# Sums of a second and third matmul operand formed from transposed tiles instead of transposed after they are formed

## The chip, the core and the metric

The kernel runs on one core of a Trainium2 chip. The metric is the device time of one execution in microseconds (us). Engines are named as the profile names them: PE is TensorE (PEld its weight load), DVE is VectorE, ACT is ScalarE, POOL is GpSimd and SP is SyncE.

## What is computed

One layer of a bidirectional encoder on 1024 tokens of width 1024, in float32:

```python
def rmsnorm(x, g):
    y = xf * lax.rsqrt(jnp.mean(xf * xf, axis=-1, keepdims=True) + NORM_EPS)
    return y * g
def swiglu(x, w_gate, w_up, w_down):
    return (jax.nn.silu(x @ w_gate) * (x @ w_up)) @ w_down
...
    h = swiglu(rmsnorm(x, ffn1_pre_g), ffn1_w_gate, ffn1_w_up, ffn1_w_down)   # 1024 -> 2816 -> 1024
    x = x + 0.5 * rmsnorm(h, ffn1_post_g)
    h = rmsnorm(x, mix_pre_g)
    qkv = (h @ w_qkv) ...                     # 16 heads of 64: 8 neighbourhood, 8 dilated
    ...
    mixed = jnp.concatenate([o_na, o_dil], axis=-1) @ w_out
    x = x + rmsnorm(mixed, mix_post_g)
    h = swiglu(rmsnorm(x, ffn2_pre_g), ffn2_w_gate, ffn2_w_up, ffn2_w_down)
    x = x + 0.5 * rmsnorm(h, ffn2_post_g)
```

Three normalised activations are multiplied with wide weights: ahead of the first feed-forward net, ahead of the q/k/v projection, and ahead of the second net. Below they are the first, the second and the third operand.

## The kernel before

**Products.** A float32 operand is kept as a high part, rounded to the type that TensorE multiplies (fp32r), and a low part, the remainder. `mm3` (L274) makes one product from three matmuls: high by high, high by low, low by high. The large products are cut into 2 by 2 blocks and done in seven passes of a Strassen scheme in Winograd's form. The seven left blocks made of an operand are A11, A12, A22 and S1 = A21 + A22, S2 = S1 - A11, S3 = A11 - A21, S4 = A12 - S2.

**Class `Operand`** makes these blocks, one row tile of 128 tokens at a time. Tiles 0 to 3 are upper ones and give A11 and A12; tiles 4 to 7 are lower ones, with the halves a1 (of A21) and a2 (of A22). For each pair of tiles, `squares` (L207) takes sums of squares on ACT (L172), writing their elements into the buffer `xn` that the normalised tile will use; there are two `xn` buffers. `scale` (L217) makes the reciprocal root on DVE by some twelve operations of about 0.2 us (L147 to L158, "the chain" below), and `tile` (L221) writes the normalised tile to `xn` (L225). An upper tile is saved to DRAM at once (L228, POOL's queue). For a lower tile, `sums` (L234) loads the upper one of the same columns back (`x1`, L242) and forms S1 to S4 in `s` on DVE (L248). With `c.deep` at 1, as it is for the second and third operand, there is one `x1` and one `s`, and the next lower tile's load is issued when the tile before has been turned to its last block.

**Turning.** `transpose_in` (L175) turns 128x512 values of a tile: four transposes on PE into one PSUM bank `trp` (L180, "a block" below), the high part from it on ACT (L181), and the low part on DVE (L182). An upper tile takes two blocks, a lower one five. `put` (L252) queues one step for each, and PE's order is written by hand: the matmul loops call `c.step()` after every second `mm3` group, which takes one pending sum and one step from their queues. The order on ACT, DVE and POOL is that in which the framework's scheduler places the instructions. Every engine runs its own list in order.

**Where the operands are made.** The second operand's upper tiles are turned inside the last passes of the first net, its lower ones inside the value and the first q/k passes. The third's upper ones are turned in the out-projection, its lower ones in `ahead` (L411), which runs the first passes of the second net by A11 and A12 while the other blocks are not there yet. In `ahead`, a product by A11 fills a PSUM bank, `save` (L443, `keep` L387) copies it out on ACT (L389) and stores it through POOL's queue, and the product by A12 is added to the same bank. Weight blocks come in through SP's queue (`graw`, L397) and are split to `whi` on ACT (L370) and `wlo` on DVE (L371). `Finish.rest` (L770) loads a tile of the residual (L778), adds the post-norm to it (L781) and stores it (L783), both through POOL's queue.

Of the kernel before, what the change touches and what calls it, by code (L numbers as in the profile page):

```python
# [10 lines left out]
F32 = mybir.dt.float32  # L11
# [8 lines left out]
P, T = 128, 512  # L20
# [9 lines left out]
A11, S2, S1, S4, A12, S3, A22 = range(7)  # L30
# [5 lines left out]
class Ctx:  # L36


    def __init__(self, tc):
        self.tc, self.nc = tc, tc.nc  # L40
        self.todo = deque()
        self.units, self.fillers = deque(), deque()
        self.left, self.rate, self.debt = 0, 0, 0
        self.steps, self.sums, self.pace = deque(), deque(), 1
# [130 lines left out]
def transpose_in(c, x, hi, lo, tag="tr", pool=None):  # L175

    nc = c.nc
    ps = (pool or c.pst).tile([P, 4, P], F32, tag=tag, name="trp")
    for j in range(4):
        nc.tensor.transpose(ps[:, j, :], x[:, j * P:(j + 1) * P], c.ident)  # L180
    nc.scalar.copy(hi, ps)  # L181
    nc.vector.tensor_sub(lo, ps, hi.bitcast(F32))  # L182


class Operand:

    def __init__(self, c, gain, which):
        self.c, self.gain, self.x, self.parts, self.wait, self.open, self.pinned = c, gain, {}, {}, deque(), 0, False  # L190
        for b in (A11, A12):
            self.x[b] = [c.xa.tile([P, 4, T], F32R, tag=f"x{b}{i}", name=f"x{b}{i}") for i in range(2)]
        self.saved = [c.dr.tile([P, D], F32, name=f"xn{which}_{t}") for t in range(4)]
# [27 lines left out]
    def tile(self, t, x, xn, r):  # L221
        c, nc = self.c, self.c.nc
        if xn is None:
            xn = c.xp.tile([P, D], F32, tag="xn", name="xn", bufs=c.xn)
        nc.vector.scalar_tensor_tensor(xn, x, r, self.gain, op0=ALU.mult, op1=ALU.mult)  # L225
        a1, a2 = xn[:, :T], xn[:, T:]
        if t < 4:
            nc.gpsimd.dma_start(self.saved[t], xn)  # L228
            self.parts[t] = deque(((A11, a1), (A12, a2)))
        else:  # L230
            self.wait.append((t, a1, a2))
            self.sums()

    def sums(self):  # L234

        c, nc = self.c, self.c.nc
        if not self.wait or self.open == c.deep:
            return
        self.open += 1
        t, a1, a2 = self.wait.popleft()  # L240
        x1 = c.xp.tile([P, D], F32, tag="x1", name="x1", bufs=c.deep)
        nc.gpsimd.dma_start(x1, self.saved[t - 4])  # L242
        s = c.xp.tile([P, 4, T], F32, tag="s", name="s", bufs=c.deep)
        a11, a12 = x1[:, :T], x1[:, T:]
        s1, s2, s3, s4 = [s[:, i, :] for i in range(4)]
        add, sub = nc.vector.tensor_add, nc.vector.tensor_sub
        for f, *args in ((add, s1, a1, a2), (sub, s2, s1, a11), (sub, s3, a11, a1), (sub, s4, a12, s2)):
            c.sums.append(lambda f=f, args=args: self.pin(lambda: f(*args)))  # L248
        parts = deque(((A22, a2), (S1, s1), (S2, s2), (S3, s3), (S4, s4)))
        c.sums.append(lambda: self.parts.__setitem__(t, parts))  # L250

    def put(self, t):  # L252

        for i in range(5 if t >= 4 else 2):
            self.c.steps.append(lambda: self.one(t))

    def one(self, t):
        while not self.parts.get(t):
            self.c.sums.popleft()()
        b, src = self.parts[t].popleft()  # L260
        cols = slice(t % 4 * P, t % 4 * P + P)
        transpose_in(self.c, src, *[h[:, :, cols] for h in self.x[b]])
        if t >= 4 and not self.parts[t]:
            self.open -= 1
            self.sums()


def load_gain(c, g, tag):
# [79 lines left out]
class PairGemm:  # L348
# [17 lines left out]
    def split(self, raw, tag, pool=None, place=None):  # L366
        c, nc = self.c, self.c.nc
        hi, lo = place() if place else [(pool or c.wr).tile(list(raw.shape), F32R, tag=tag + p, name="w" + p)
                                        for p in ("hi", "lo")]
        nc.scalar.copy(hi, raw)  # L370
        nc.vector.tensor_sub(lo, raw, hi.bitcast(F32))  # L371
        return hi, lo
# [113 lines left out]
    def run(self, final=None, ahead=None):  # L486
# [3 lines left out]
        for b in range(self.n):  # L490
            w, early = self.w.pop(b), b < self.early
            direct, second, sums, rest = self.prepare(b + 1)
            if early:
                s1 = sp.tile([P, T], F32, tag="s1", name="s1")
# [233 lines left out]
class Finish:  # L728
# [22 lines left out]
    def end(self, t, h):  # L751

        c, nc = self.c, self.c.nc
        x, (q, k) = self.xt[t - 4], [self.q[:, i, t - 4:t - 3] for i in range(2)]
        y, v, e = [c.small.tile([P, 4], F32, tag=n, name=n)[:, :1] for n in ("y", "v", "e")]
        nc.vector.tensor_scalar(q, self.ss[:, t, 1:2], 1.0 / D, EPS, op0=ALU.mult, op1=ALU.add)
        nc.scalar.activation(y, self.ss[:, t, 0:1], AF.Sqrt, bias=q, scale=1.0 / D)
        nc.vector.tensor_scalar(k, q, -0.5, None, op0=ALU.mult)
        nc.vector.scalar_tensor_tensor(v, self.ss[:, t, 0:1], -0.5 / D, k, op0=ALU.mult, op1=ALU.add)
        nc.vector.reciprocal(y, y)  # L760
        nc.vector.scalar_tensor_tensor(e, y, v, y, op0=ALU.mult, op1=ALU.mult)
        nc.vector.scalar_tensor_tensor(y, e, 1.5, y, op0=ALU.add, op1=ALU.mult)
# [193 lines left out]
class Unit:  # L956
# [15 lines left out]
    def turn(self):  # L972
        c = self.c
        self.tps = c.pst.tile([P, 4, P], F32, tag="tr", name="ptp")
        for j in range(self.n):
            c.nc.tensor.transpose(self.tps[:, j, :], self.probs[:, j * P:(j + 1) * P], c.ident)  # L976
# [300 lines left out]
def layer(tc, a, out):  # L1277
    nc = tc.nc
    c = Ctx(tc)
    with ExitStack() as ctx:  # L1280
# [3 lines left out]
        def sub():  # L1284
            return ctx.enter_context(ExitStack())
# [18 lines left out]
        x1 = [c.dr.tile([P, D], F32, name=f"x1_{t}") for t in range(8)]  # L1304
# [6 lines left out]
        def right(w, ts, where):  # L1311

            def get(i):
                q = {k: ts[i][j] for j, k in enumerate((T1, T3, T2, T4))}
                for (g, u), k in zip(((0, 0), (0, 1), (1, 1)), (B11, B21, B22)):
                    ch = where(i)[u]
                    q[k] = w[g, ch // 2][:, ch % 2 * T:ch % 2 * T + T]
                return q
            return get
# [144 lines left out]
        s1, s2, xas = sub(), sub(), sub()  # L1464
# [3 lines left out]
        with ExitStack() as order:  # L1468
# [6 lines left out]
                    xs[t] = c.xp.tile([P, D], F32, tag="x", name="x", bufs=4)  # L1475
                    q.dma_start(xs[t], x0[t])
            xs = {}
            op0 = Operand(c, None, 0)

            def begin(pg):  # L1480
                row, eps, ss = c.xp.tile([P, D + P], F32, tag="s", name="row", bufs=2), *[
# [284 lines left out]
        s7, s3, s4, s5 = sub(), sub(), sub(), sub()  # L1766
# [203 lines left out]
```

## Time and profile before

| | before |
|---|---|
| median of 3 runs (lowest to highest) | 1868.24 us (1865.01 to 1870.01) |
| the profiled execution, and its span | 1868.1 us, 1866.1 us |
| PE busy | 1838.7 us (99%) |
| PEld busy | 1534.3 us (82%) |
| DVE busy | 1318.9 us (71%) |
| ACT busy | 795.5 us (43%) |
| POOL busy | 324.8 us (17%) |

Busy is the time in which at least one instruction of the engine ran; the span runs from the first to the last instruction. Matmuls overlap each other: one takes about 0.39 us and the next starts 0.23 us after it. The share of PE is one over the whole program, so what a change is worth has to be read at the place where it stands.

### The profile page before, as it was taken

The numbers are of one execution on the slowest core, as the hardware profiler recorded it, in microseconds if no ns is written. First come the engines' busy times: TensorE is split into PE (matmuls) and PEld (weight loads), VectorE is DVE, ScalarE is ACT, GpSimd is POOL, SyncE is SP. The second block draws the span as 40 slices with busy tenths as digits, with TensorE's granted clock in tenths as the row PEclk, the third lists the DMA queues.
The fourth block names the chain that finished last, engine by engine and source line by source line (L and its number), as shares of the span: only waits on it lengthen the run. The fifth ranks groups of instructions, "written<-read, shape, count | busy, mean of one in ns | idle before, by whom it ended". The sixth has DMA issues, their size and how long they took to land.

```text
span 1866.1 us, 25121 instructions
## 1 busy us (share of the span) xinstructions
PE 1838.7 (99%) x9048; PEld 1534.3 (82%) x9048; DVE 1318.9 (71%) x2208; ACT 795.5 (43%) x1300; POOL 324.8 (17%) x521
## 2 busy tenths in 40 slices
PE   8999999999999999999999999999999999999998
PEld 6888878888888887888899988778888888888886
DVE  6778776777565877577766766785878777754557
ACT  5522233334443645233477765453222333344333
POOL 2101221223000122222442300121111111110000
PEclk9999999999999999999999999999999999999999
DMA  7655467788986756656883732585455656586564
GB/s 267 226 172 192 154 210 240 227 250 274 343 288 210 269 189 225 230 160 222 295 288 111 249 137 81 193 297 175 158 191 184 239 207 233 193 319 206 195 225 148
DMA packets 164990, 404.63 MB, mean 217 GB/s; under 512 B 18881, under 2 KB 35489, under 8 KB 162818
## 3 DMA queue, kind: packets, MB, share of 16 engines
q1 hardware_dynamic: 115664, 228.30, 36.9%
q0 software_dynamic: 48336, 172.63, 26.5%
q10 hardware_dynamic: 866, 2.10, 0.3%
q8 instruction: 71, 1.16, 0.3%
q14 instruction: 53, 0.43, 0.1%
HBM read 276.95 MB, written 131.07 MB: 219 GB/s over the span
## 4 chain that ended last, share of the span: by engine, by line
PE 81%; issue 10%; DVE 4%; DMA 2%; ACT 2%; POOL 0%; DVEq 0%; ACTq 0%; SPq 0%; POOLq 0%
PE mmp L276 17%; PE mmp L278 17%; PE mmp L277 17%; PE accp L276 7%; PE accp L278 7%; PE accp L277 7%; PE po L1088 3%; PE ptp L976 2%; PE po L1209 1%; PE trp L180 1%; PE sp L1076 1%; PE sp L1196 1%; DMA xn<-xn 0%; DMA sgd<-sg 0%; DVE x L182 0%
## 5 line engine op out<-in xcount | busy, mean ns | idle before, releaser
L276 PE MATMUL mmp<-x,whi 128*128 128x512 f32 x1412 | 559.0, 396 | 3.3 <-DVE v L507 1.8
L278 PE MATMUL mmp<-x,wlo 128*128 128x512 f32 x1412 | 553.7, 392 | 0.0
L277 PE MATMUL mmp<-x,whi 128*128 128x512 f32 x1412 | 552.3, 391 | 0.2 <-DVE x L1551 0.2
L276 PEld LDWEIGHTS mmp<-x,whi 128*128 128x128 f32 x1412 | 265.1, 188 | 62.8 <-issue 5.7
L278 PEld LDWEIGHTS mmp<-x,wlo 128*128 128x128 f32 x1412 | 264.9, 188 | 61.0 <-DVE wlo L371 0.7
L277 PEld LDWEIGHTS mmp<-x,whi 128*128 128x128 f32 x1412 | 265.2, 188 | 57.3 <-DVE x L1551 0.5
L648 DVE TENSOR_TENSOR pw<-praw,pw 128x1024 fp32r<-128x1024 f32 (+1 forms) x182 | 199.0, 1138 | 124.5 <-ACT pw L647 124.1
L370 ACT CAST whi<-wraw 128x1024 fp32r<-128x1024 f32 x126 | 132.2, 1052 | 336.1 <-PE mmp L277 276.0
L647 ACT CAST pw<-praw 128x1024 fp32r<-128x1024 f32 (+1 forms) x182 | 169.0, 982 | 204.0 <-PE accp L278 157.6
L276 PE MATMUL accp<-pw 128*128 128x512 f32 x600 | 234.4, 391 | 0.7 <-DVE hb L719 0.7
L278 PE MATMUL accp<-pw 128*128 128x512 f32 x600 | 233.5, 389 | 0.0
L277 PE MATMUL accp<-pw 128*128 128x512 f32 x600 | 233.4, 389 | 0.0
L371 DVE TENSOR_TENSOR wlo<-wraw,whi 128x1024 fp32r<-128x1024 f32 x126 | 154.4, 1227 | 20.2 <-ACT whi L370 20.1
L276 PEld LDWEIGHTS accp<-pw 128*128 128x128 f32 x600 | 112.6, 188 | 24.4 <-issue 1.1
L278 PEld LDWEIGHTS accp<-pw 128*128 128x128 f32 x600 | 112.6, 188 | 23.5
L277 PEld LDWEIGHTS accp<-pw 128*128 128x128 f32 x600 | 112.7, 188 | 23.2
L580 POOL DMA_DIRECT2D g<-sg x44 | 24.1, 547 | 410.7 <-DVE sg L573 232.6
L389 ACT COPY s<-mmp 128x512 f32<-128x512 f32 x52 | 30.6, 588 | 131.0 <-PE mmp L278 121.1
L182 DVE TENSOR_TENSOR x<-trp,x 128x512 fp32r<-128x512 f32 x76 | 52.1, 687 | 26.2 <-ACT x L181 26.1
L181 ACT CAST x<-trp 128x512 fp32r<-128x512 f32 x76 | 44.5, 587 | 46.1 <-PE trp L180 46.1
L461 DVE TENSOR_TENSOR wraw<-wraw 128x1024 f32<-128x1024 f32 x52 | 63.4, 1220 | 0.7
L536 DVE TENSOR_TENSOR c<-mmp,u 128x512 f32<-128x512 f32 x52 | 35.7, 686 | 38.6 <-PE mmp L278 38.5
(288 smaller groups left out, 2789.6 us busy)
## 6 DMA issues: line engine op xcount, KB each, us to landing
praw<-g SPq DMA_DIRECT2D x70, 512.0 KB
wraw<-in_wg_dram SPq DMA_DIRECT2D x44, 512.0 KB
wraw<-in_wu_dram SPq DMA_DIRECT2D x44, 512.0 KB
tr<-in_wd_dram SPq DMA_DIRECT2D x44, 512.0 KB
g<-sg POOLq DMA_DIRECT2D x88, 256.0 KB, 4.5
ts<-tr POOLq DMA_DIRECT2D x22, 1024.0 KB, 4.9
praw<-ts SPq DMA_DIRECT2D x88, 256.0 KB
praw<-in_wd_dram SPq DMA_DIRECT2D x66, 256.0 KB
```

Of the source, the lines that this page charges most:

```text
L181: nc.scalar.copy(hi, ps)
L182: nc.vector.tensor_sub(lo, ps, hi.bitcast(F32))
L276: nc.tensor.matmul(out, ahi, bhi, start=start, stop=False, skip_group_check=go_on)
L277: nc.tensor.matmul(out, ahi, blo, start=False, stop=False, skip_group_check=go_on)
L278: nc.tensor.matmul(out, alo, bhi, start=False, stop=stop, skip_group_check=go_on)
L370: nc.scalar.copy(hi, raw)
L371: nc.vector.tensor_sub(lo, raw, hi.bitcast(F32))
L461: nc.vector.tensor_sub(r[:, 0:2], r[:, 1:3], r[:, 0:2])
L647: nc.scalar.copy(w[side][:, 0, :m], raw[:, :m])
L648: nc.vector.tensor_sub(w[side][:, 1, :m], raw[:, :m], w[side][:, 0, :m].bitcast(F32))
L976: c.nc.tensor.transpose(self.tps[:, j, :], self.probs[:, j * P:(j + 1) * P], c.ident)
L1088: nc.tensor.matmul(po[0][:, un * 2 + j], u.pt[:, 2 * j + t, :], rhs, start=t == 0, stop=t == 1)
```

## The change

It applies to the second and the third operand (`turned=True`); the first is built with `turned=False` and goes on as before.

- An upper tile's block is copied back on ACT from PSUM into `xn` in its transposed form, and the save to DRAM is issued after both blocks, so that what is saved is the transposed tile.
- A lower tile is turned in two blocks in place of five: `left` turns a1 and takes S3 from PSUM, `right` turns a2, splits A22, and forms S2, S1 and S4 on DVE from the turned values. The four sums are split afterwards from `s` in SBUF: high part on ACT, low part on DVE.
- The next lower tile's `x1` is loaded after S4 of the tile before; its sums cannot be formed before its turn on PE. `put` queues two steps and two empty ones for a lower tile.

```diff
         if t < 4:
-            nc.gpsimd.dma_start(self.saved[t], xn)
-            self.parts[t] = deque(((A11, a1), (A12, a2)))
+            if not self.turned:
+                nc.gpsimd.dma_start(self.saved[t], xn)
+            self.parts[t] = deque(lambda b=b, src=src: self.plain(t, b, src) for b, src in ((A11, a1), (A12, a2)))
+            if self.turned:
+                self.parts[t].append(lambda: nc.gpsimd.dma_start(self.saved[t], xn))
...
+    def split(self, t, b, src):
+        nc = self.c.nc
+        hi, lo = self.cols(t, b)
+        nc.scalar.copy(hi, src)
+        nc.vector.tensor_sub(lo, src, hi.bitcast(F32))
+
+    def plain(self, t, b, src):
+        ps = self.turn(src)
+        self.split(t, b, ps)
+        if self.turned:
+            self.c.nc.scalar.copy(src.rearrange("p (k c) -> p k c", k=4), ps)
...
+        def left():
+            while self.splits:
+                c.sums.popleft()()
+            new = place()
+            s.extend(new[:, i].rearrange("p (k c) -> p k c", k=4) for i in range(4))
+            sub(s[2], a11, self.turn(a1))
+
+        def later(b, x):
+            self.splits -= 1
+            self.pin(lambda: self.split(t, b, x))
+
+        def right():
+            s1, s2, s3, s4 = s
+            ps = self.turn(a2)
+            self.split(t, A22, ps)
+            sub(s2, ps, s3)
+            add(s1, s2, a11)
+            sub(s4, a12, s2)
+            self.end()
+            self.splits = 4
+            c.sums.extend(lambda b=b, x=x: later(b, x) for b, x in ((S2, s2), (S3, s3), (S1, s1), (S4, s4)))
+        self.parts[t] = deque((left, right))
...
-        for i in range(5 if t >= 4 else 2):
+        for i in range(5 if t >= 4 and not self.turned else 2):
             self.c.steps.append(lambda: self.one(t))
+        if t >= 4 and self.turned:
+            self.c.steps.extend([lambda: None] * 2)
```

Line numbers differ between the two programs: in the changed one the transposes are L244, the split L250 and L251, the copy back L257, the late save L233, the reload L267, the sums L290 to L302, the weight splits L431 and L432, the copy of `keep` L450, the residual's lines L839 to L844, and the q/k rotation L981 (before: L920). Three places show how the order on the engines moves.

First, POOL's queue in the out-projection, where the third operand's upper tiles 0 and 1 (`xn2_0`, `xn2_1`) are saved and the residual's tiles 2 and 3 (`x2_2`, `x2_3`) are stored. Before:

```order
L228 DMA xn2_0_10768<-xn_11033 128x1024
L228 DMA xn2_1_10769<-xn_11034 128x1024
L783 DMA x2_2_103<-x_11061 128x1024
L783 DMA x2_3_104<-x_11062 128x1024
L242 DMA x1_11460<-xn2_0_10768 128x1024
```

The changed kernel:

```order
L233 DMA xn2_0_10716<-xn_10981 128x1024
L844 DMA x2_2_103<-x_11009 128x1024
L844 DMA x2_3_104<-x_11010 128x1024
L233 DMA xn2_1_10717<-xn_10982 128x1024
L267 DMA x1_11416<-xn2_0_10716 128x1024
```

The save of tile 1 has moved behind the stores of residual tiles 2 and 3.

Second, ACT's list at the start of `ahead`. `trp_11284` (now `trp_11238`) is the last block of the upper tile 3; the `whi` are high parts of the first weight blocks; `s1` is the copy of the first product by A11 out of its PSUM bank; the activation into `xn` is the square of tile 4. Before:

```order
L181 CAST x40_10766<-trp_11284 128x4x128
L370 CAST whi_11324<-graw_11189 128x1024
L370 CAST whi_11367<-graw_11263 128x1024
L389 COPY s1_11344<-mmp_11330 128x512
L370 CAST whi_11410<-graw_11328 128x1024
L172 ACTIVATE xn_11424,ss_11423<-x_11363 128x1024
L389 COPY s1_11387<-mmp_11373 128x512
```

The changed kernel:

```order
L431 CAST whi_11280<-graw_11141 128x1024
L431 CAST whi_11323<-graw_11216 128x1024
L257 COPY xn_11115<-trp_11238 128x512
L431 CAST whi_11366<-graw_11284 128x1024
L172 ACTIVATE xn_11380,ss_11379<-x_11319 128x1024
L450 COPY s1_11300<-mmp_11286 128x512
```

The first copy of `s1` stood behind two weight splits; it stands now behind three, the copy back of tile 3 and the square of tile 4.

Third, DVE's list where the second operand's tiles 6 and 7 get their chain, ahead of the turning of tile 6. `x31` is the low part of block S4 of tile 5, `qk` a product of an earlier pass, `wlo` low parts of weights. Before:

```order
L371 TENSOR_TENSOR wlo_5834<-graw_5739,whi_5833 128x1024
L147 TENSOR_SCALAR v_5864<-ss_5846 128x2
L148 TENSOR_SCALAR y_5865<-v_5864 128x2
L149 TENSOR_SCALAR y_5865<-y_5865 128x2
L182 TENSOR_TENSOR x31_5431<-trp_5851,x30_5430 128x4x128
L156 TENSOR_TENSOR e_5866<-y_5865,v_5864 128x2
```

The changed kernel:

```order
L251 TENSOR_TENSOR x21_5433<-s_5762,x20_5432 128x4x128
L147 TENSOR_SCALAR v_5876<-ss_5823 128x2
L432 TENSOR_TENSOR wlo_5862<-graw_5753,whi_5861 128x1024
L981 TENSOR_TENSOR qk_5856<-qk_5856 128x512
L251 TENSOR_TENSOR x31_5439<-s_5762,x30_5438 128x4x128
L148 TENSOR_SCALAR y_5877<-v_5876 128x2
```

After the chain's first operation (L147) there stand now a weight split, a q/k product and a low part, and the other eleven operations come behind them; before, the chain went on at once with one low part in between.

## Rows read from the trace of the kernel before

**Rows 1.** The page: engines and TensorE clock.

```profile
PE 1838.7 (99%) x9048; PEld 1534.3 (82%) x9048; DVE 1318.9 (71%) x2208; ACT 795.5 (43%) x1300; POOL 324.8 (17%) x521
...
PEclk9999999999999999999999999999999999999999
```

**Rows 2.** Waits of PE: engine, line, releaser: us in total, times, longest.

```profile
PE trp L180 <- DVE xn L225: 2.3, 2, 1.7
...
PE trp L180 <- DVE s L248: 1.5, 1, 1.5
...
PE trp L180 <- DVE x L182: 1.1, 4, 0.4
```

**Rows 3.** Timeline of PE at third operand's tile 2: start, us, instruction.

```profile
1206.91 0.39 PE L278 MATMUL accp<-whi,n 128*128 128x512 f32 x1
...
1207.14 0.60 PE L180 MATMUL trp<-ident,xn 128*128 128x128 f32 x4
...
1207.82 0.39 PE L277 MATMUL accp<-wlo,n 128*128 128x512 f32 x1
```

**Rows 4.** Timeline of PE at second operand's tile 6; idle before in brackets.

```profile
720.02 0.63 PE L180 MATMUL trp<-ident,xn 128*128 128x128 f32 x4 [0.56 <-DVE xn L225]
...
723.55 0.63 PE L180 MATMUL trp<-ident,s 128*128 128x128 f32 x4 [1.52 <-DVE s L248]
```

**Rows 5.** Timeline of ACT and DVE ahead of that tile.

```profile
717.85 1.05 ACT L370 CAST whi<-graw 128x1024 fp32r<-128x1024 f32 x1 [1.26 <-PE mmp L277]
...
719.44 0.62 ACT L919 CAST qk<-qk 128x512 fp32r<-128x512 f32 x1
...
720.99 0.68 DVE L920 TENSOR_TENSOR qk<-qk 128x512 fp32r<-128x512 f32 x1
...
721.59 1.22 DVE L371 TENSOR_TENSOR wlo<-graw,whi 128x1024 fp32r<-128x1024 f32 x1
...
723.33 0.68 DVE L182 TENSOR_TENSOR x<-trp,x 128x512 fp32r<-128x512 f32 x1
```

**Rows 6.** Timeline of ACT, DVE and POOL around the third operand's upper saves.

```profile
1200.08 1.06 ACT L172 ACTIVATE xn<-x 128x1024 f32<-128x1024 f32 x1 [1.70 <-DMA xn<-xn]
...
1201.32 1.06 ACT L172 ACTIVATE xn<-x 128x1024 f32<-128x1024 f32 x1
...
1198.86 1.29 DVE L781 SCALAR_TENSOR_TENSOR x<-hs,y,x 128x1024 f32<-128x1024 f32 x1 [1.00 <-DMA x<-x]
...
1202.50 0.17 DVE L147 TENSOR_SCALAR v<-ss 128x2 f32<-128x2 f32 x1 [1.76 <-ACT xn L172]
...
1204.88 1.29 DVE L225 SCALAR_TENSOR_TENSOR xn<-x,y,gain 128x1024 f32<-128x1024 f32 x1
...
1193.78 1.07 POOL L228 DMA_DIRECT2D xn<-xn  x2
```

**Rows 7.** Line L228, the saves: issue to landing.

```profile
DMA to landing us min/median/max: 4.4/5.2/6.9
```

**Rows 8.** Timeline of ACT and PE at the start of the third operand's passes.

```profile
1216.00 0.59 ACT L389 COPY s<-mmp 128x512 f32<-128x512 f32 x1
...
1219.99 1.05 ACT L370 CAST whi<-graw 128x1024 fp32r<-128x1024 f32 x1 [3.41 <-DMA graw<-in_wg_dram]
...
1220.95 1.06 ACT L172 ACTIVATE xn<-x 128x1024 f32<-128x1024 f32 x1
...
1218.73 0.39 PE L276 MATMUL mmp<-x,w 128*128 128x512 f32 x1
```

**Rows 9.** Timeline of PE, DVE and ACT at second operand's tile 2.

```profile
657.66 0.60 PE L180 MATMUL trp<-ident,xn 128*128 128x128 f32 x4
...
655.45 2.48 DVE L225 SCALAR_TENSOR_TENSOR xn<-x,y,gain 128x1024 f32<-128x1024 f32 x2
...
639.72 1.05 ACT L647 CAST pw<-praw 128x1024 fp32r<-128x1024 f32 x1
```

**Rows 10.** Line L242, the reloads: issue to landing.

```profile
DMA to landing us min/median/max: 4.3/6.0/10.5
```

More of the change, by code (lines that the diff above doesn't have):

```diff
@@ L185, with __init__ @@
 class Operand:
-    def __init__(self, c, gain, which):
+    def __init__(self, c, gain, which, turned=True):
         self.c, self.gain, self.x, self.parts, self.wait, self.open, self.pinned = c, gain, {}, {}, deque(), 0, False
+        self.turned, self.splits = turned, 0
         for b in (A11, A12):
@@ L232, in tile, with cols, turn @@
             self.sums()
+    def cols(self, t, b):
+        return [h[:, :, t % 4 * P:t % 4 * P + P] for h in self.x[b]]
+    def turn(self, src):
+        ps = self.c.pst.tile([P, 4, P], F32, tag="tr", name="trp")
+        for j in range(4):
+            self.c.nc.tensor.transpose(ps[:, j, :], src[:, j * P:(j + 1) * P], self.c.ident)
+        return ps
+    def split(self, t, b, src):
[8 more added lines that the diff above has]
+            self.c.nc.scalar.copy(src.rearrange("p (k c) -> p k c", k=4), ps)
     def sums(self):
@@ L242, in sums @@
         nc.gpsimd.dma_start(x1, self.saved[t - 4])
-        s = c.xp.tile([P, 4, T], F32, tag="s", name="s", bufs=c.deep)
-        a11, a12 = x1[:, :T], x1[:, T:]
-        s1, s2, s3, s4 = [s[:, i, :] for i in range(4)]
         add, sub = nc.vector.tensor_add, nc.vector.tensor_sub
-        for f, *args in ((add, s1, a1, a2), (sub, s2, s1, a11), (sub, s3, a11, a1), (sub, s4, a12, s2)):
-            c.sums.append(lambda f=f, args=args: self.pin(lambda: f(*args)))
-        parts = deque(((A22, a2), (S1, s1), (S2, s2), (S3, s3), (S4, s4)))
@@ L250, in sums, with place @@
-        c.sums.append(lambda: self.parts.__setitem__(t, parts))
+        def place():
+            return c.xp.tile([P, 4, T], F32, tag="s", name="s", bufs=c.deep)
+        if not self.turned:
+            s = place()
+            a11, a12 = x1[:, :T], x1[:, T:]
+            s1, s2, s3, s4 = [s[:, i, :] for i in range(4)]
+            for f, *args in ((add, s1, a1, a2), (sub, s2, s1, a11), (sub, s3, a11, a1), (sub, s4, a12, s2)):
+                c.sums.append(lambda f=f, args=args: self.pin(lambda: f(*args)))
+            parts = deque(lambda b=b, src=src: self.plain(t, b, src)
+                          for b, src in ((A22, a2), (S1, s1), (S2, s2), (S3, s3), (S4, s4)))
+            c.sums.append(lambda: self.parts.__setitem__(t, parts))
+            return
@@ new lines, in sums @@
+        a11, a12 = [x1[:, i * T:i * T + T].rearrange("p (k c) -> p k c", k=4) for i in range(2)]
+        s = []
+        def left():
[17 more added lines that the diff above has]
+            c.sums.extend(lambda b=b, x=x: later(b, x) for b, x in ((S2, s2), (S3, s3), (S1, s1), (S4, s4)))
@@ L252, in put, with end @@
+        self.parts[t] = deque((left, right))
+    def end(self):
+        self.open -= 1
+        self.sums()
     def put(self, t):
-        for i in range(5 if t >= 4 else 2):
+        for i in range(5 if t >= 4 and not self.turned else 2):
             self.c.steps.append(lambda: self.one(t))
+        if t >= 4 and self.turned:
+            self.c.steps.extend([lambda: None] * 2)
     def one(self, t):
@@ L259, in one @@
             self.c.sums.popleft()()
[L260 to L265, printed above, removed]
+        self.parts[t].popleft()()
+        if t < 4 and self.turned and len(self.parts[t]) == 1:
+            self.parts[t].popleft()()
+        if t >= 4 and not self.turned and not self.parts[t]:
+            self.end()
 def load_gain(c, g, tag):
@@ L1477, in layer @@
             xs = {}
-            op0 = Operand(c, None, 0)
+            op0 = Operand(c, None, 0, False)
             def begin(pg):
```

## Prediction

> **What bounds the kernel now.** I read the page first. PE is busy for 99% of the span, at a granted clock that stays at the upper of its two levels (2.4 GHz) in every slice [rows 1]. A PE instruction that falls away is therefore worth its time, and a wait of PE costs its length, unless something else was already holding PE there. DVE (71%) and ACT (43%) have room on average, but the average says nothing of the few us around a row tile. So I went next to the waits of PE: for the blocks of transposes (L180) only small ones are left, 2.3 us for a normalised tile, 1.5 for a sum and 1.1 for a low part that still had to be read out of the PSUM bank [rows 2]. Last I read the timeline at the places where the order of the changed program differs, engine by engine, and followed there what would come late.
>
> **What the change removes.** Eight lower tiles lose three blocks each: 24 blocks. One block in the stream of matmuls costs the distance between the matmul ahead of it and the second one behind it, 1207.82 - 1206.91 = 0.91 us, less two matmul steps of 0.227: 0.455 us [rows 3]. 24 of them are 10.9 us. Waits fall away with them: the 1.52 for a sum and the 0.56 for a normalised tile at the second operand's tile 6 [rows 4], and of the four waits of 1.1 us for low parts about 0.7 (three of the four stand in the third operand) [rows 2]. The 1.7 for the third operand's first tile stays. Together 10.9 + 2.8 = 13.7 us, which is the gain if nothing comes late.
>
> **What it adds at no cost.** Sixteen copies on ACT: no row of before shows one; the nearest is the high part taken from the same bank, and the s1 copy of the same size takes 0.59 us [rows 8]. That is 9.4 us on an engine that is busy for 43%, and it costs nothing by itself; what it costs is order. The lower tiles' DVE work keeps its number of operations.
>
> **What it makes late.** Five places; at each I take what waits, and from when.
>
> First, the second operand's tile 6. PE wanted it at 720.02 - 0.56 = 719.46 [rows 4]. In the changed order the chain for tiles 6 and 7 stands behind a weight low part, whose high part on ACT starts at 717.85, because PE releases its buffer only then, and ends at 718.90, and behind a q/k product, whose ACT part ends at 720.06 [rows 5]. From 718.9 on: low part 1.22 to 720.1, q/k 0.68, low part of S4 0.68 [rows 5] to 721.5, eleven operations of the chain at 2.38 / 12 = 0.2 (twelve run from 1202.50 to 1204.88) [rows 6] to 723.7, normalised tile 1.28 (as L225 takes, 2.48 for two less what overlaps) [rows 9] to 725.0. Stall 5.5 us; at least 3, if the S4 part or the product goes elsewhere, at most 7.
>
> Second, the third operand's tile 2, which PE wanted at 1207.14 [rows 3]. The square of tile 3 writes the `xn` buffer of tile 1 and so waits for that tile's save. Before, the saves were issued at 1193.78, and the square of tile 2 started at 1200.08, on the landing [rows 6]. Now tile 1's save follows both blocks, both copies, and in POOL's queue the store of residual tile 3, whose DVE part ends at 1198.86 + 1.29 = 1200.15. The low part of tile 1's second block comes behind that on DVE (0.69), the copy behind the low part (0.59): save at 1201.4. Landing takes 5.2 (4.4 to 6.9) [rows 7]: 1206.6. Then square 1.06 and its read-out to 1207.9, chain 2.4 with one residual product between (0.7), to 1211.1, tile 1.28: 1212.4. Stall 5.2; 4.4 with the shortest landing, 7 with the longest, 3 if the copy does not wait for the low part and the store.
> The Trainium skill, "DMA: Bandwidth & Descriptors", section "Anatomy of one DMA", puts a transfer from POOL's queue at about 2.0 us and its bytes over 436 GB/s; for 512 KB that is an estimate of 3.2 us. The trace disagrees: 4.4 is the least of eight. By the page this term would be 3.2 in place of 5.2.
>
> Third, the start of `ahead`. The product by A12 is added to the bank that the first s1 copy must read, and PE starts it at 1218.73; the copy was done at 1216.59 [rows 8]. Now that copy stands behind the third weight split and the square of tile 4. The split waits for its load until 1219.99, then 1.05 and 1.06 us for split and square bring 1222.0, with the read-out 1222.2, and the copy 0.59 more [rows 8]. PE goes on at about 1223.1: stall 4.4. If the load came 2 us earlier, 2.4; 6 if the square waits for the save of tile 2.
>
> Fourth, the second operand's tile 2, wanted at 657.66; its normalised tile was ready at 655.45 + 1.28 = 656.7 [rows 9]. Tile 0's second copy stands behind a weight split that ended at 640.77 [rows 9], so save 0 goes out at about 641.4 and lands at 646.6 [rows 7]; only then run the square of tile 2 and, behind it on ACT, tile 1's second copy (1.2 and 0.6), and save 1 follows at 648.5. It lands 5.2 later, and square, chain and tile (4.9) with a weight split between (0.7) end at about 659.4. Stall 1.7, take 2.0; 0 to 3.4.
>
> Fifth, the reloads of `x1`. Blocks of one tile are 1.83 us apart (two groups of `mm3`, 1.37, and a block). The next reload is issued after S4 of the tile before: second block 1.83, high part 0.59, low part and three sums at 0.69, some 5.2 us after that tile's first block. The next tile's first block follows 2 x 1.83 + 2 x 1.37 = 6.4 us after it, so a landing of 6.0 (4.3 to 10.5) [rows 10] holds DVE at S3 for about 4.8 us. PE feels of that only what a weight low part behind it comes late, some 6 us of landing later: 0 at the median, 4.5 at the longest. For three such places and for two low parts queued behind the sums I take 4 together; 0 to 9.
>
> **The sum.** 1868.1 - 13.7 + 5.5 + 5.2 + 4.4 + 2.0 + 4.0 = 1875.5 us. The profiled execution is 0.1 us from the median of the runs, so nothing is added for that. 0.3%, about what a measurement of this kernel can tell from no change, is 5.6 us: the stalls decide at 8.1 (below it faster) and 19.3 (above it slower); I have 21.1.
>
> **The rivals.**
> The transfers land quickly. With the shortest rows, 4.4 and 4.3, the second term is 4.4, the fourth 1.2, the fifth some 1.5 (the two low parts): 1868.1 - 13.7 + 5.5 + 4.4 + 4.4 + 1.2 + 1.5 = 1871.4, no measurable change. For it: the place of the fifth is a median that just hides. Against it: DMA is busy around these places, and eight saves never took less. Chance 0.30, with any other way in which a third of the stalls is hidden (1863 to 1873). The page of the Trainium skill named above would make the landings shorter still, and lead into this rival.
> One stall absorbs the next. PE waiting gives ACT, DVE and the queues time, so that of each operand only the longest wait is paid: 5.5 and 5.2, in all 10.7, 1865.1. If the weight buffer ahead of tile 6 is free 2.6 us earlier (its split idled 1.26 for PE [rows 5]), tile 6 costs 2.9, and it is 1862.5, faster; at no stall 1854.4. Against it: each of the waits hangs on something that PE itself releases or that follows PE's own blocks, so a late PE makes it late too. Chance of ending below 1862.6: 0.17.
> Landings at their longest, 6.9 and 10.5, bring 7, 3.4 and 9 in the second, fourth and fifth terms: 1884 us. Chance 0.08.
>
> **How the numbers follow.** The forecast, five stalls at about their size and slower by 3 to 14 us, has 0.45, its own range 1871 to 1882; with the longest landings, slower holds 0.53. No change 0.30, faster 0.17. The range leaves out the lower part of the faster case and the upper end of the slower one: 1861 to 1885.
>
> **What would show it.** Right: 96 transposes fewer among PE's 9048 instructions [rows 1]; waits of PE for the normalised tile of 5 us or so at two places, and one of some 4 us for the s1 copy. Steps wrong: if the waits of L244 are under 2 us, the saves or the chain are not late; if PE's wait for the s1 copy is missing, ACT was not held. The prediction fails if these three are together under 8 us, or if a stall stands somewhere that none of the five names.

## The result and the profile after

The changed kernel takes 1878.9 us in the median of four runs (1875.96 to 1881.64); before takes 1869.12 in four runs (1865.01 to 1870.09). The ratio is 1.0058, with a 95% interval of 1.0045 to 1.007: slower by 9.8 us in the medians. The forecast was 1875.5 and slower, range 1861 to 1885.

The page of the changed kernel, busy time of each engine and the granted TensorE clock by slices, answers to [rows 1]:

```profile
PE 1835.4 (98%) x8952; PEld 1528.1 (81%) x8952; DVE 1318.4 (70%) x2208; ACT 803.0 (43%) x1316; POOL 323.9 (17%) x521
...
PEclk9999999999999999999999999999999999999999
```

PE runs 96 fewer transposes and is busy 3 us less, and the program is nevertheless longer: the difference is idle time of PE. The tenths of the clock still read 9 in every slice; slices of 47 us are too coarse for what is shown below. The waits of PE in the changed kernel (engine, line, releaser; us in total, times, longest) answer to [rows 2]; L244 are the transposes, L450 is the s1 copy, L337 and L338 are matmuls:

```profile
PE trp L244 <- DVE xn L226: 11.6, 4, 5.5
...
PE mmp L337 <- ACT s L450: 5.6, 2, 4.4
...
PE accp L338 <- DVE pw L709: 1.3, 2, 0.8
...
PE accp L337 <- ACT pw L708: 0.9, 1, 0.9
PE mmp L339 <- DVE pw L432: 0.8, 1, 0.8
...
PE trp L244 <- DVE x L251: 0.4, 1, 0.4
```

Waits for a normalised tile went from 2.3 us to 11.6, and one for an s1 copy appeared with 4.4; those for sums of a lower tile are gone, and those for low parts of the operand shrank to one, in the first operand. The wait of 0.8 us for a weight's low part (L432) is new; it comes some 6 us after the second operand's tile 4 has been turned. Two lines on the value weights (`pw`) are new too: they stand at the hand-off from the q/k passes to the value passes, which no term of the sum had:

```profile
755.55 0.50 PE L338 MATMUL accp<-pw,x 128*128 128x512 f32 x1 [0.52 <-DVE pw L709]
...
757.86 0.50 PE L337 MATMUL accp<-pw,x 128*128 128x512 f32 x1 [0.88 <-ACT pw L708]
...
759.12 0.50 PE L338 MATMUL accp<-pw,x 128*128 128x512 f32 x1 [0.76 <-DVE pw L709]
```

To see where the time went, each matmul of the changed program was laid beside the same one of the kernel before (transposes left out), and the distance between their starts read at the ends of each operand's stretch. The distance grows from 3.2 to 7.9 us over the second operand (the matmuls that before start between 630 and 762) and from 7.0 to 12.8 over the third (1185 to 1300). So the second cost 4.7 us and the third 5.7, in this one run. The first 3.2 us arise in the first net, where the change adds nothing; other runs of the same code show from -0.2 to 5.5 us there, so it is taken for scatter and not for the change. An idle time of PE shows in these distances with some 0.16 us more than its length, since the matmuls on its two sides, which else overlap (0.39 us long, 0.23 apart), no longer do: the 0.52 and 0.88 us above appear as 0.68 and 1.04.

### The profile page after: what moved, and what is told of

It reads as the page before. It is cut to its first block, busy times and chain, and to the rows that moved or that the text cites. A ratio compares the mean times of both kernels' runs of the same rounds, so it can differ in the third digit from the quotient of the medians.

```text
span 1877.8 us, 24958 instructions
## 1 busy us (share of the span) xinstructions
PE 1835.4 (98%) x8952; PEld 1528.1 (81%) x8952; DVE 1318.4 (70%) x2208; ACT 803.0 (43%) x1316; POOL 323.9 (17%) x521
## 4 chain that ended last, share of the span: by engine, by line
PE 82%; DMA 9%; DVE 5%; ACT 2%; issue 2%; SPq 0%; DVEq 0%; POOL 0%; ACTq 0%; POOLq 0%
PE mmp L337 14%; PE mmp L339 14%; PE mmp L338 14%; PE accp L338 10%; PE accp L339 10%; PE accp L337 10%; DMA tr<-in_wd_dram 4%; PE po L1149 3%; DMA ts<-tr 2%; PE ptp L1037 2%; PE po L1270 1%; PE sp L1137 1%; PE trp L244 1%; DMA xn<-xn 1%; PE sp L1257 1%
## 5 line engine op out<-in xcount | busy, mean ns | idle before, releaser
L337 PE MATMUL mmp<-x,whi 128*128 128x512 f32 x1412 | 558.6, 396 | 4.7 <-ACT u L450 1.4
L338 PE MATMUL mmp<-x,whi 128*128 128x512 f32 x1412 | 553.0, 392 | 0.2 <-DVE x L1612 0.2
L337 PEld LDWEIGHTS mmp<-x,whi 128*128 128x128 f32 x1412 | 265.3, 188 | 67.3 <-issue 5.4
L338 PEld LDWEIGHTS mmp<-x,whi 128*128 128x128 f32 x1412 | 265.4, 188 | 58.1 <-DVE x L1612 0.5
L431 ACT CAST whi<-wraw 128x1024 fp32r<-128x1024 f32 x126 | 132.2, 1051 | 325.3 <-PE mmp L338 254.2
L337 PE MATMUL accp<-pw 128*128 128x512 f32 x600 | 234.2, 390 | 0.0
L338 PE MATMUL accp<-pw 128*128 128x512 f32 x600 | 233.4, 389 | 0.0
L432 DVE TENSOR_TENSOR wlo<-wraw,whi 128x1024 fp32r<-128x1024 f32 x126 | 153.6, 1221 | 17.6 <-ACT whi L431 17.5
L337 PEld LDWEIGHTS accp<-pw 128*128 128x128 f32 x600 | 112.6, 188 | 23.3
L338 PEld LDWEIGHTS accp<-pw 128*128 128x128 f32 x600 | 112.6, 188 | 23.1
L450 ACT COPY s<-mmp 128x512 f32<-128x512 f32 x52 | 30.5, 587 | 125.6 <-PE mmp L339 115.9
L402 DVE TENSOR_TENSOR tr<-tr 128x1024 f32<-128x1024 f32 x26 | 31.8, 1221 | 48.1 <-DMA tr<-in_wd_dram 40.8
L431 ACT CAST whi<-traw 128x512 fp32r<-128x512 f32 x52 | 32.2, 620 | 55.0 <-DVE traw L523 55.0
```

The source lines that it names most:

```text
L337: nc.tensor.matmul(out, ahi, bhi, start=start, stop=False, skip_group_check=go_on)
L338: nc.tensor.matmul(out, ahi, blo, start=False, stop=False, skip_group_check=go_on)
L402: nc.vector.tensor_sub(r[:, 0:2], r[:, 1:3], r[:, 0:2])
```

## The experiments

All ratios are to the kernel before in the same set of runs; the changed kernel has four runs, the others four to twelve. The last two columns are the growth of that distance over the two stretches, from the one profiled run of each kernel, where a few tenths are not meaningful. The hand-off alone takes 2.7 to 3.0 us of the second column wherever the second operand is changed, and more in two runs: 4.6 with the s1 copy first and 5.0 with tile 6 later.

| run | median us | ratio (95%) | second operand | third operand |
|---|---|---|---|---|
| changed kernel | 1878.9 | 1.0058 (1.0045 to 1.0070) | +4.7 | +5.7 |
| third operand as before | 1872.9 | 1.0025 (1.0016 to 1.0034) | +4.6 | -0.1 |
| second operand as before | 1874.1 | 1.0032 (1.0021 to 1.0043) | 0.0 | +6.0 |
| chain first | 1876.3 | 1.0045 (1.0034 to 1.0057) | 0.0 | +6.8 |
| s1 copy first | 1883.7 | 1.0084 (1.0071 to 1.0097) | +7.8 | +9.5 |
| squares into x1 | 1876.2 | 1.0036 (1.0025 to 1.0048) | +4.1 | +0.6 |
| chain first, squares into x1 | 1871.9 | 1.0020 (1.0010 to 1.0029) | -0.9 | +1.1 |
| all three | 1869.3 | 1.0006 (0.9996 to 1.0015) | +1.0 | +0.8 |
| all three, two x1 | 1869.1 | 1.0001 (0.9991 to 1.0010) | 0.0 | -1.0 |
| the same, tile 6 later | 1866.8 | 0.9987 (0.9978 to 0.9995) | -0.9 | -0.3 |

**The third operand as before.** One operand at a time is built in the old way.

```diff
-            op = Operand(c, g3, 2)
+            op = Operand(c, g3, 2, False)
```

> The third operand is built as before, the second stays changed. Laying the two traces side by side matmul by matmul, the changed program is 7.1 us behind ahead of the third operand and 11.9 behind at its end, so the third operand alone costs 4.8 us. Theory (the loss is a few waits of PE at named places: tile 2, the s1 copy): the time falls by 4 to 6 us from 1878.9, to about 1874, ratio to before about 1.0026, and the waits of 4.0 us for tile 2 and 4.45 us for the s1 copy are gone from the trace. Rival (the change earns in the third operand, and the loss is a general slowing by copies and transfers, such as the 3 us that the profiled run of the changed kernel loses in the first net where nothing is changed): the time stays within 2 us of 1878.9 or rises.

It fell by 6.0 us in the medians, and both waits are gone from its trace: the loss of the third operand is local to it.

**The second operand as before.**

```diff
-                op = fin.op = Operand(c, gain, which)
+                op = fin.op = Operand(c, gain, which, False)
```

> The second operand is built as before, the third stays changed. By the same alignment the changed program is 3.0 us behind ahead of the second operand and 7.7 behind after it (5.5 us of wait at tile 6, 2.2 at the first products behind the q/k passes, against 12 blocks saved). Theory: 1878.9 falls by 3 to 6 us, to about 1874, ratio about 1.0027, and the wait at tile 6 goes back to 0.6 and 1.5 us. Rival (general slowing, or the second operand about even): within 2 us of 1878.9.

It fell by 4.8 us, and 0.56 and 1.50 us are back at tile 6. The two ratios add up to that of the whole change (0.25% and 0.32% against 0.58%): within the intervals, no general slowing is left to explain.

**Chain first.** The chain and the normalised tiles no longer queue behind the splits of the tile before.

```diff
-        self.c.sums.append(lambda: self.scale(*n))
+        getattr(self.c.sums, "appendleft" if self.turned else "append")(lambda: self.scale(*n))
...
+        if self.turned:
+            self.c.sums.extendleft(reversed(tiles))
+        else:
+            self.c.sums.extend(tiles)
```

> As changed, but the operation that makes the reciprocal root, and the normalised tiles behind it, go to the front of the queue of pending sums, ahead of the four splits of the tile before. Theory (tile 6 is late because its chain stands on DVE behind those splits, a weight low part and a product): in the order only the weight low part is left ahead of the normalised tile, PE's wait at tile 6 falls from 5.5 to 2 us or less, and the time by 3 to 5 us to about 1875, ratio about 1.003; the stretch at the lower granted clock behind the wait goes with it. Rival (the wait is handed on: the splits that now come later hold PE at the next passes): wait at tile 6 shorter, time within 1.5 us of 1878.9.

PE's timeline of that kernel at the second operand's tile 6:

```profile
723.05 0.63 PE L247 MATMUL trp<-ident,xn 128*128 128x128 f32 x4 [2.45 <-DVE xn L229]
```

The wait went from 5.53 to 2.45 us, where 2 or less was expected. The median fell by 2.6 us, less than the 3 to 5 expected, and the intervals of the two ratios overlap. In the profiled runs the stretch of the second operand fell by 4.7: 3.1 of wait, and 1.7 of matmuls at the lower clock behind it (granted clock 1.00 from 723 to 726 us here, 0.50 behind the wait of 5.53). The mechanism is as said; its size in time lies between the two.

**The s1 copy first.** The third weight split and the squares of tiles 4 and 5 are issued behind the first s1 copy.

```diff
+            marks = self.first if b == 3 else []
+            self.c.after(marks, lambda: self.w.__setitem__(b, self.split(self.raw.pop(b), "g", None, self.place.get(b))))
...
                 self.save(b, a)
+                if b == 0 and 0 in self.place and 3 not in self.place:
+                    self.first = self.op.first = c.marks(ACT)
...
-        n = self.squares(ts, xs)
+        n = []
+        self.c.after(self.first, lambda: n.extend(self.squares(ts, xs)))
```

> As changed, but at the start of the third operand's passes the third weight split and the squares of tiles 4 and 5 are issued on ACT behind the first s1 copy. Theory (PE waits 4.45 us there only because ACT runs those two ahead of the copy): the wait is gone, with the 1.7 us that the matmuls behind it lose at the lower granted clock, and the time falls by 4 to 6 us, to about 1874, ratio about 1.0025. Rival (the copy waits for something else, or the split that now comes later holds PE one product on): a wait of 2 us or more stays within 10 us of that place, and the time falls by under 2 us.

The rival was right that the wait is handed on, though not in its terms: no single wait of 2 us stays, and the time rose by 4.8 us in the medians. The waits of PE in that kernel: the 4.4 us are gone, and waits for weight parts stand in their place (L434 and L433 are the weight splits, L452 the s1 copy; the totals hold waits in other stretches too):

```profile
PE mmp L340 <- DVE wlo L434: 3.8, 3, 1.8
...
PE mmp L338 <- ACT s L452: 2.1, 2, 1.1
...
PE mmp L338 <- ACT whi L433: 1.5, 2, 1.2
```

In the third operand PE now waits 1.06, 1.44, 1.18 and 1.80 us, 5.5 in all. The last two come within 3 us of each other some 30 us after the s1 copy, and then the granted clock is down (columns: the window, its length, busy time and number of instructions of PE, PEld, DVE, ACT and POOL, granted clock, DMA share, GB/s):

```profile
1272.90:1278.00 5.10, 5.06 (x12) 4.01 (x13) 4.72 (x16) 1.77 (x3) 1.08 (x2) 0.50 0.81 275
```

So the wait was passed on, not removed, and the kernel came out slower than the changed one. The second operand's stretch of this run, which the edit does not touch, is 3 us longer too, half of it at the hand-off; how much of the 4.8 us is due to the edit stays open.

**Squares into x1.** The squares of tiles 2 and 3 go to a buffer that nobody reads, so that they do not wait for the saves.

```diff
-        n = self.squares(ts, xs)
+        junk = self.c.xp.tile([P, D], F32, tag="x1", name="junk", bufs=self.c.deep) if self.turned and 2 in ts else None
+        n = self.squares(ts, xs, junk)
```

> As changed, but the squares of the upper tiles 2 and 3 are written to the buffer x1, not to the xn buffers, so that they no longer wait for the saves of tiles 0 and 1; only the normalised tile 3 then needs the landing of save 1. Theory (the square behind the late save is what makes tile 2 late in the third operand, 4.0 us, and the 2.1 us of PE time lost right behind it are the lower granted clock): the wait for tile 2 falls to under 1 us, the time by 4 to 6 us, to about 1874, ratio about 1.0025. Rival (PE waits instead for tile 3, or the reload into x1 becomes late): the wait moves by one tile, and the time falls by under 2 us.

The waits of PE that are left for s1 copies and normalised tiles:

```profile
PE mmp L338 <- ACT s L451: 8.0, 2, 4.8
...
PE trp L245 <- DVE xn L227: 7.1, 2, 5.6
```

Of the normalised tiles only the second operand's tile 6 (5.6) and the third's first (1.5) still wait: the 3.97 us for the third's tile 2 and the 0.59 for the second's are gone, and not handed to tile 3. (Of the 8.0 us for s1 copies, 4.8 stand in the third operand and 3.1 in the first net.) The theory's waits went as it said. The third operand's stretch fell by 5.1 us, but the medians by 2.7 only, short of the 4 to 6 expected.

**All three together.**

> The three edits together: chain first, s1 copy first, squares of tiles 2 and 3 into x1. Theory (the three waits of 5.5, 4.0 and 4.45 us and the stretches at the lower granted clock behind them, 1.0, 2.1 and 1.7 us, are the loss, and the blocks saved are worth 10.9 us): 13 to 16 us less than 1878.9, so 1863 to 1866, ratio 0.997 to 0.9985, faster than before. Rival (a wait removed is handed on to the next place): 1870 or more.

It is 9.6 us below the changed kernel and even with the kernel before, where 13 to 16 were expected: the theory of waits that simply add was too simple. What took their place in the third operand is in the timelines of DVE, ACT and PE of that kernel (L295 is S3, L255 a high part, L438 and L437 are the weight splits, L342 and L344 matmuls):

```profile
1253.69 0.69 DVE L295 TENSOR_TENSOR s<-x,trp 128x512 f32<-128x512 f32 x1 [5.87 <-DMA x<-xn]
...
1257.37 1.22 DVE L438 TENSOR_TENSOR wlo<-graw,whi 128x1024 fp32r<-128x1024 f32 x1
...
1254.41 0.62 ACT L255 CAST x<-s 128x512 fp32r<-128x512 f32 x1 [4.24 <-DVE s L295]
1254.94 1.04 ACT L437 CAST whi<-graw 128x1024 fp32r<-128x1024 f32 x1
...
1256.03 0.50 PE L342 MATMUL mmp<-x,whi 128*128 128x512 f32 x1 [1.18 <-ACT whi L437]
...
1258.64 0.50 PE L344 MATMUL mmp<-x,wlo 128*128 128x512 f32 x1 [1.87 <-DVE wlo L438]
```

DVE stands 5.87 us at S3 of tile 5, since the reload of x1 has not landed. On ACT the high part of S3 waits for it, and the weight's high part stands behind that; on DVE the weight's low part runs only at 1257.37. PE waits 1.18 and 1.87 us for the two. With 1.63 us for a weight's low part some 20 us earlier, these are 4.7 us of waits in the place of 4.45.

In the changed kernel the same S3 waited 2.25 us only. There the reload landed 4.8 us after its issue, here 8.4, with the DMA engines fully busy in both (share 1.04 and 1.03). The same holds over the nine kernels that change the third operand, for the reload issued behind tile 4. Where PE waits 4 us and more for the s1 copy it takes 4.8 to 5.0 us in four kernels and 7.0 in a fifth; in the four where PE waits 1.1 us or less it takes 7.8 to 8.4. So the reload was quicker where PE stood still.

In the second operand, tile 6's wait of 2.49 us is followed by a lower clock here (0.75), which the like wait of 2.45 us with the chain alone was not (columns as above):

```profile
721.90:724.50 2.60, 2.54 (x11) 2.05 (x12) 2.60 (x4) 0.00 (x0) 0.59 (x1) 0.75 0.92 351
```

**Without the s1 edit.** All three, less the edit on the s1 copy.

```diff
-                    self.first = self.op.first = c.marks(ACT)
+                    pass
```

> The chain first and the squares of tiles 2 and 3 into x1, without the edit on the s1 copy. All three edits together came to 1869.3, and the s1 edit by itself made the changed kernel slower (1883.7), with waits of 1.1 to 1.8 us at four later places in the place of the one of 4.45. Theory A (the s1 wait is real and its 4.45 us and 1.7 us of lower clock come back here, while the later waits for weight parts fall away): between 1869 and 1873. Theory B (the wait is only handed on, so that the s1 edit is worth nothing in either combination, or costs 3 to 5 us as it did by itself): 1865 to 1869, no slower than with all three.

1871.9, as theory A has it: 2.6 us above all three together in the medians, though the intervals overlap. The profiled runs say less: the third operand's stretch grows by 1.1 us with the wait of 4.64 and by 0.8 without it. Taking away a wait of 4.6 us at that place thus gave 0.3 us in the profiled stretches and 2.6 in the medians, the rest being passed on; how much of the 2.6 is scatter stays open.

**Two x1 buffers.** On top of all three, the third operand gets two x1 buffers.

```diff
-        if not self.wait or self.open == c.deep:
+        if not self.wait or self.open == self.deep:
...
-        x1 = c.xp.tile([P, D], F32, tag="x1", name="x1", bufs=c.deep)
+        x1 = c.xp.tile([P, D], F32, tag="x1", name="x1", bufs=self.deep)
...
-            op = Operand(c, g3, 2)
+            op = Operand(c, g3, 2, deep=2)
...
-            early_pools(e)
+            early_pools(e, 3 - (which == 3))
```

> All three edits, and for the third operand two x1 buffers in place of one, so that the next lower tile's reload no longer waits for S4 of the tile before; to make room the pool for the s1 copies of those passes has two buffers in place of three. In the run with the three edits DVE stood 5.87 us at S3 of tile 5, waiting for the reload, and PE then waited 1.18 and 1.87 us for a weight block split late. Theory (the fifth term of the prediction: a reload that lands late holds DVE, and the weight parts queued behind it hold PE): those two waits are gone, with what the lower clock costs behind them, 3 to 5 us less than 1869.3, so 1864 to 1866, ratio about 0.998. Rival (PE waits there for the weight load itself, or the pool with two buffers costs as much): within 1.5 us of 1869.3.

The median is unchanged (1869.1), as the rival has it. In the profiled run DVE's 5.87 us at S3 of tile 5 are gone (0.1), the two waits of 1.18 and 1.87 us became 0.59 and 0.57, and the stretch is 1.8 us shorter, with one new wait of 1.0 for a weight high part. The mechanism is there; a gain in time is not shown. What the smaller pool costs was not separated.

**Tile 6 later.** What was left largest in the second operand was the wait of 2.5 us.

```diff
-            plan(8, {1: [A(6, 7), U(5)], 3: [U(6)], 5: [U(7)]}, False)
+            plan(8, {1: [A(6, 7), U(5)], 4: [U(6)], 5: [U(7)]}, False)
```

> As the kernel with two x1 buffers, and the second operand's tile 6 is turned one product later, so that PE comes to it 2.8 us later. In that kernel's run the normalised tile 6 is ready 2.5 us after PE wants it. Theory: the wait of 2.5 us is gone, and the time falls by 2 to 3 us, to 1866 to 1867, ratio to before about 0.9985. Rival (tile 6 is late for the hand-off to the value passes instead, where the loads wait for the buffers of the operand: 0.5, 0.6 and 0.8 us of PE waits there already): the waits there grow, and the time stays within 1 us of 1869.1.

The waits of PE for normalised tiles, and at the hand-off for the value weights:

```profile
PE accp L343 <- ACT pw L718: 2.2, 1, 2.2
...
PE trp L250 <- DVE xn L232: 1.5, 1, 1.5
```

Only the third operand's first tile (1.5 us) still waits for its normalised tile. The hand-off took much of it back, as the rival said it might: its waits grew by 1.0 us (2.2 and 0.8, after 0.5, 0.6 and 0.8), and behind them the granted clock fell (0.66 from 752 to 755 us), so that by the distances it costs 2.3 us more than with two x1 buffers alone; the second operand's stretch is 0.9 us shorter. At 0.9987 this is the one version of the ten that beats the kernel before, by 2.1 us in the medians (0.5 to 2.2 in a thousand). Its interval overlaps that of the version before it, so what the later tile 6 gives by itself is not shown.

## Why the prediction was right

It had the sign and most of the size, 7.4 of 9.8 us. Its signs of being right came: 96 transposes fewer, waits of 5.5 and 4.0 us for normalised tiles and one of 4.4 for the s1 copy. But one of its signs of failing came too, a stall at a place that none of its five terms names: the hand-off, with 2.2 us of waits. The number held; the list of what makes it up was not complete. By its own steps:

**What is removed.** PE's instructions fell by 96, and where no wait stands the distance to the kernel before falls by 0.4 to 0.5 us at each block that is missing, as 0.455 says. The waits for low parts, 0.7 of them in the sum, are gone from the third operand. The gain of about 13.7 us was there, and was spent.

**First, tile 6, 5.5 us.** ACT, DVE and PE of the changed kernel at that place answer to [rows 4, 5]:

```profile
720.35 1.06 ACT L431 CAST whi<-graw 128x1024 fp32r<-128x1024 f32 x1
...
721.93 0.62 ACT L980 CAST qk<-qk 128x512 fp32r<-128x512 f32 x1
...
721.43 1.23 DVE L432 TENSOR_TENSOR wlo<-graw,whi 128x1024 fp32r<-128x1024 f32 x1
...
722.58 0.69 DVE L981 TENSOR_TENSOR qk<-qk 128x512 fp32r<-128x512 f32 x1
...
723.19 0.68 DVE L251 TENSOR_TENSOR x<-s,x 128x512 fp32r<-128x512 f32 x1
...
723.79 0.16 DVE L148 TENSOR_SCALAR y<-v 128x2 int32<-128x2 int32 x1
...
726.04 1.28 DVE L226 SCALAR_TENSOR_TENSOR xn<-x,y,gain 128x1024 f32<-128x1024 f32 x1
...
727.47 1.09 PE L244 MATMUL trp<-ident,xn 128*128 128x128 f32 x4 [5.53 <-DVE xn L226]
...
730.92 0.78 PE L244 MATMUL trp<-ident,xn 128*128 128x128 f32 x4
...
731.46 0.48 PE L337 MATMUL mmp<-x,pw 128*128 128x512 f32 x1
```

High part at 720.35, low part, product and S4 part on DVE until 723.8, eleven operations of the chain, the tile at 726.04, and PE at 727.47 after 5.53 us. The order of the sum is there row by row. Putting the chain first took 3.1 us off the wait. Behind the wait the work of PE itself was slower: the tile's second four transposes, at 730.92, took 0.78 us, where before they took 0.63 [rows 4].

**Second, the third operand's tile 2, 5.2 us.** POOL, ACT, DVE and PE answer to [rows 6]:

```profile
1207.27 0.53 POOL L844 DMA_DIRECT2D x<-x  x1 [1.25 <-DVE x L842]
...
1208.53 0.53 POOL L233 DMA_DIRECT2D xn<-xn  x1 [0.73 <-ACT xn L257]
...
1207.65 0.59 ACT L257 COPY xn<-trp 128x512 f32<-128x512 f32 x1 [0.76 <-DVE x L251]
...
1212.61 1.06 ACT L172 ACTIVATE xn<-x 128x1024 f32<-128x1024 f32 x1 [1.86 <-DMA xn<-xn]
...
1213.80 0.17 DVE L147 TENSOR_SCALAR v<-ss 128x2 f32<-128x2 f32 x1 [2.32 <-ACT xn L172]
...
1216.64 2.48 DVE L226 SCALAR_TENSOR_TENSOR xn<-x,y,gain 128x1024 f32<-128x1024 f32 x2
...
1218.07 0.63 PE L244 MATMUL trp<-ident,xn 128*128 128x128 f32 x4 [3.97 <-DVE xn L226]
```

PE stood 3.97 us. In the frame of the kernel before (this run is 6.8 us behind there, by PE's first block at 1198.48) the save of tile 1 is issued at 1201.7, as worked out (1201.4), behind the store and the copy; it landed in some 4.0 us where 5.2 was taken. Sending the squares elsewhere removed the wait. All saves of the changed kernel, from issue to landing, against [rows 7]:

```profile
DMA to landing us min/median/max: 2.9/3.1/5.2
```

A median of 3.1 us, where the sum took the 5.2 of the saves of before; this one save took 4.0, and the 1.2 us between are about the whole error of the term. The saves now go out one by one, where before each pair went out within 1.2 us; whether that or the other traffic made them quicker no run separates. The Trainium skill, "DMA: Bandwidth & Descriptors", section "Anatomy of one DMA", gave an estimate of 3.2 us for this size. By it the term would have been 3.2, and 3.97 was measured; the prediction set it aside because the saves of before never took less than 4.4, and for the saves of the changed kernel it was nearer.

**Third, the s1 copy, 4.4 us.** ACT and PE answer to [rows 8]:

```profile
1233.68 1.04 ACT L431 CAST whi<-graw 128x1024 fp32r<-128x1024 f32 x1 [4.31 <-DMA graw<-in_wg_dram]
...
1234.64 1.05 ACT L172 ACTIVATE xn<-x 128x1024 f32<-128x1024 f32 x1
...
1235.69 0.57 ACT L450 COPY s<-mmp 128x512 f32<-128x512 f32 x1
...
1236.31 0.68 PE L337 MATMUL mmp<-x,w 128*128 128x512 f32 x1 [4.45 <-ACT s L450]
```

4.45 us, by the steps of the sum: the load at 1233.68, split, square, copy. The size was right, but not what it is worth: the experiments that remove it pass most of it on. The reload of tile 5 takes 3.6 us longer without it (8.4 after 4.8), and weight parts come late.

**Fourth, the second operand's tile 2, 2.0 us.** 0.59 was measured; for this term, too, the landing was taken too long.

**Fifth, reloads and low parts, 4 us.** In the changed kernel it came to 0.8 us. That is PE's wait at 700.25 us for a weight's low part, which stands on DVE behind the sums and a low part of tile 4, as the term says of low parts. The reload held DVE for 2.25 us and PE for nothing that shows. With the waits ahead of it removed it held DVE for 5.87 and cost PE 3.05 us. The term was real but largely hidden behind the others, as the rival of absorption says for one place.

**What the sum did not have.** The hand-off, 2.2 us, and the clock: 1.7 us of slower work of PE behind each of the three large waits, 5.1 in all (the last section). The waits named came to 5.5 + 4.0 + 4.5 + 0.6 = 14.6 of the 17.1 forecast for the first four terms, and to 0.8 of the 4.0 for the fifth; the two unnamed costs, 7.3, made up for that and more. All together less the gain, 14.6 + 0.8 + 7.3 - 13.7, is 9.0 of the 10.4 us by which the two stretches grew; the rest is in small things such as the 0.16 us at the edges of each wait. The forecast's nearness is in part an accident: 5.7 us too much in its own terms, 7.3 left out.

**The rivals.** Quick landings was half right: they were quicker, and the result still slower. Absorption held in the third operand between the s1 copy and the reload, not between tile 2 and the s1 copy. Saves at their longest did not come.

## What to carry to other kernels

When a change takes work off an engine at 99%, look first for the places at which it also changes the order on the other engines: here 24 blocks worth 11 us were paid back by a queue of pending work that put a normalisation chain behind splits, a save behind a store, and a copy behind a load. A wait that is removed is worth only what the next late thing leaves of it: here one of 4.6 us gave way to three of 4.7 in all. Count the chain of waits again with the first one gone. An edit that moves work on a shared in-order queue is checked best in the order of instructions, before any time is asked for.

## What the runs showed of the hardware that was not expected

After the waits of 4.0 to 5.5 us, PE's granted clock stood at the lower level, 1.2 GHz, for about the next 3 us of matmuls. Windows behind the three large waits of the changed kernel, and two ordinary ones (columns: the window, its length, busy time and number of instructions of PE, PEld, DVE, ACT and POOL, granted clock, DMA share, GB/s):

```profile
727.50:730.50 3.00, 3.00 (x10) 2.52 (x11) 1.88 (x2) 0.62 (x1) 0.00 (x0) 0.50 0.18 70
...
733.00:743.00 10.00, 10.00 (x47) 8.15 (x46) 8.24 (x13) 6.38 (x10) 2.43 (x4) 1.00 0.44 157
...
1218.00:1222.00 4.00, 3.93 (x16) 3.33 (x17) 2.42 (x3) 2.40 (x5) 1.06 (x2) 0.67 0.54 154
...
1236.30:1240.30 4.00, 3.99 (x11) 3.14 (x12) 2.55 (x13) 2.76 (x4) 1.09 (x2) 0.57 0.84 280
...
1241.00:1246.00 5.00, 5.00 (x23) 4.04 (x22) 1.76 (x2) 1.14 (x2) 2.17 (x4) 1.00 0.71 238
```

0.50, 0.67 and 0.57 where the others have 1.00; matmuls start 0.43 us apart instead of 0.23. By the distances to the kernel before this cost 1.7 us behind each of the three, on top of the waits themselves, 0.3 to 0.4 of the length of each. (The expectations above have 1.0, 2.1 and 1.7: the first leaves out the slowed transposes, the second takes in a wait of 0.2 us and its edges.) Not only long waits did it: in the kernel with the s1 copy first, two waits of 1.18 and 1.80 us within 3 us were followed by the window at 0.50 shown above. Nor does the length of a wait settle it: behind 2.45 us at tile 6 the clock was 1.00 (chain first), behind 2.49 at the same place 0.75 (all three), and behind the three short waits of the hand-off 1.00 in the changed kernel and 0.59 (760 to 764 us) with the s1 copy first. What decides between them no run separates.

Two things stay open. The first is the hand-off, the one stall that no term had. The value weights' loads on SP start later there: the first at 743.7 us after 735.7, the third at 750.6 after 743.0, while the program as a whole is some 6 us behind at the first and 5 at the third, so about 2 us of each is new. SP's own waits in that stretch are put down to the transposes of the operand (L244, 13.2 us, until those of tile 7 end) and to a low part of it (L251, 5.8 us). That fits loads which wait for the buffers of the operand to be free; no run moves them alone. The second is the scatter of -0.2 to 5.5 us in the first net of the profiled runs. Much of it stands at PE's wait for the first s1 copy some 45 us after the start, 1.1 to 3.8 us long, and in the changed kernel at waits of 1.42 and 0.74 us at 411 and 459 us; why these vary was not looked for.
